# Attention of a hybrid decoder layer, written in units of 128 keys with the projection stream between them

## The chip, the cores and the metric

The kernel runs on one core of one Trainium2 chip. The metric is device microseconds of one execution; the median of several runs counts. One further execution was recorded by the hardware profiler, and all rows below come from it.

## The reference

One decoder layer for 512 tokens of width 1024: two token mixers side by side (HGRN2, a gated recurrence, and NSA, a sparse attention), merged by gates, followed by an MLP. The change touches the attention and the projections that are computed beside it. With 512 tokens and blocks of 64 keys the top-16 selection takes every block, and the window of 512 covers every earlier token, so that the selected and the window branch are both causal softmax attention over all earlier keys, with keys and values of their own (ks, vs and kw, vw).

```python
def reference(x, ...):
    u = rms_norm(h, norm_pre_mix[i])
    proj = u @ w_in[i]
    hq, hf, hi, hg, nq, nkv, ngate, ga, gb = jnp.split(proj, SPLIT_POINTS, axis=-1)
    kc, vc, ks, vs, kw, vw = jnp.split(nkv, 6, axis=-1)
    y_a = hgrn2_mixer(hq, hf, hi, hg, ...)
    y_b = nsa_mixer(nq, kc, vc, ks, vs, kw, vw, ngate, ...)
...
def nsa_mixer(...):                      # 16 heads in 4 groups of 4, 64 wide
    s = jnp.einsum('bgrqd,bgnd->bgrqn', qb, k_cmp)      # compressed keys
    o_cmp = jnp.einsum('bgrqn,bgnd->bgrqd', masked_softmax(s, ...), v_cmp)
    s = jnp.einsum('bgrqd,bgqkd->bgrqk', qr, kg)        # selected keys
    o_sel = jnp.einsum('bgrqk,bgqkd->bgrqd', masked_softmax(s, m_sel), vg)
    s = jnp.einsum('bgrqd,bgkd->bgrqk', qr, kwb)        # window
    o_win = jnp.einsum('bgrqk,bgkd->bgrqd', masked_softmax(s, m_win), vwb)
    out = gt[:, :, 0] * o_cmp + gt[:, :, 1] * o_sel + gt[:, :, 2] * o_win
```

## The kernel before

**Precision.** A float32 operand is held as two tiles of a faster type, a high part (`hi`) and the rest (`lo`). A product of two such operands takes three matmuls, a triple (hi·hi, lo·hi, hi·lo). Making the pair costs a copy on ScalarE (ACT) and a subtraction on VectorE (DVE): `split`, L59 and L60. During the attention weights are made into pairs in another way, `split_by_transfer`, L62 to L65: two copies on ACT and a transfer with accumulation, issued on GpSimd's queue (POOL).

**The main stream.** `job_n` (L136) multiplies the 512 normalised tokens (`uh`, `ul`) with 256 columns of `w_in`: four token tiles t, each with eight k-steps of a triple with 256 columns, in a PSUM bank of the pool `mainp` (two banks). It needs two chunks of weights. `job_t` (L129) makes 128 columns transposed: eight k-steps of a triple with 512 columns, one chunk. Three chunks can live at a time (`PAIRS`), and two raw ones (`RAWS`). Beside the attention run five `job_n` (queries of groups 1 to 3; keys and values of the second pair of groups, twice) and eight `job_t` (`gate_tanh`, L218).

**The attention.** `attend` (L469) does one of four groups of heads as a generator of eight steps: for each tile t of 128 queries the two branches. `scores` (L472) of a step: matmuls against t+1 tiles of keys, the maximum on DVE (L488), the exponentials on ACT (L492), the scaling (L502, L505). `values` (L508): for each of the t+1 tiles of keys four transposes of the probabilities (L169), the split into `pth` and `ptl` (ACT, then DVE), and two matmuls (L515, L516). One such tile of keys is called a unit here: 20 in a group, 80 in all. The scores of a step are written ahead of the values of the step before it. At the end of a t stands one more matmul (L542) and `store`.

**Pieces.** A group's queries and keys are made ready by short pieces: `tr_r` (L351) transposes into a `mainp` bank and a copy to SBUF (keys L379, queries L415), two more transposes (L424), the compressed scores with their softmax (`cmp_soft`, L431), and four times transposes and a split of their probabilities (`cmp_probs`, L455).

**Order.** The framework plans each engine's order ahead of time: among the instructions that are ready in the plan it takes the one that is written first in the program. An engine then executes in that order. `mark` (L76) notes matmuls of the attention, and `spread` (L79) puts the first matmul of each k-step of the stream behind one of them, in proportion: a bound on how early it may come. From L618 the program writes some steps of the attention first, then a few jobs of the stream, spread over these steps, then the pieces of the next group, and so on; the last steps of one group are written alternating with the first steps of the next (`advance`, L611). The list of marks is not emptied before this part, so that the first job, `kv(1, 0)`, is spread over marks of the stage ahead of the attention too. The attention's PSUM banks come free when those of the stage ahead (`prp`) are released, after the last `cmp_probs` of group 0.

Of the kernel before, what the change touches and what calls it, by code (L numbers as in the profile page):

```python
# [19 lines left out]
NT = 4  # L20
NK = 8
# [7 lines left out]
def hybrid_layer(ctx: ExitStack, tc: tile.TileContext, x, p, w_in, w_branch_a, w_branch_b, w_out,  # L29
# [120 lines left out]
    def n_chunks(w, cols, rows=(4, 4)):  # L150
        res, k = [], 0
# [206 lines left out]
    def kv_job(pr, ck, cv, kdst, vdst, chunks=None):  # L358
# [16 lines left out]
        job_n(chunks or n_chunks(w_in, [(ck + pr * 128, 128), (cv + pr * 128, 128)]),  # L375
              (uh, ul), mainp, evac)
        for j in range(2):
            for src, dst, e in ((hn, KH, 0), (ln, KL, 1)):
                ps = tr_r([src[:, t, j] for t in range(NT)])  # L379
                kt = kdst[2 * j + e]  # L380
                if e:
                    act.copy(kt, ps.bitcast(FT))
                else:
                    dve.tensor_copy(kt, ps)
                dst.append(kt)
        return KH, KL, V

    def q_job(g):
        return q_rest(*q_main(g))

    def q_main(g):
        qsn = ns.tile([128, NT, 4, 128], FR, name="stage", bufs=1)
# [14 lines left out]
        cols = [(C_NQ + g * 256, 256)]  # L407
        job_n(n_chunks(w_in, cols) if g else n_chunks(w_in, cols + [(C_GATE, 48)], (3, 3, 2)),
# [3 lines left out]
    def q_rest(qsn, qn):  # L412
        qs = [ns.tile([128, 512], FR, name="qs", tag="qs", bufs=8) for _ in range(4)]
# [6 lines left out]
        qt = []  # L420
# [8 lines left out]
        return qs, qt  # L429

    def cmp_soft(g, qt):  # L431
# [6 lines left out]
        sc = ns.tile([128, NT, 4, 32], FT, name="sc")  # L438
# [16 lines left out]
    def cmp_probs(sc):  # L455
        chl = []
# [10 lines left out]
        return chl  # L467

    def attend(g, qs, chl, kvs):  # L469
# [38 lines left out]
        def values(t, br, Ps, py):  # L508
            V = kvs[br][2]
            for kt in range(t + 1):  # L510
# [5 lines left out]
                mark(pe.matmul(py, V[j][:, kt], lo, start=False, stop=False), 1.0)  # L516

        def store(t, py):
# [16 lines left out]
        for i, (t, br) in enumerate(steps):  # L535
# [3 lines left out]
            values(t, br, pend, py)  # L539
# [736 lines left out]
```

## Time and profile before

| what | us |
|---|---|
| median of 3 runs (1232.16 to 1237.37) | 1235.8 |
| the profiled execution | 1233.28 |
| its span, first to last instruction | 1231.5 |
| the attention in it, first score to last value matmul | 136.5 to 411.5 |

The profile lists for each engine when it was busy. PE is TensorE's matmul, PEld its weight loads. A matmul's row has its whole duration, although the next one starts before it ends: the interval from one start to the next is the time that a stream of matmuls takes. Behind a row or group stands the idle time of the engine before it, and what ended that.

### The profile page before, as it was taken

What the parts mean: (1) busy time and instruction counts of PE and PEld (TensorE: products, weight loads), DVE (VectorE), ACT (ScalarE), POOL (GpSimd) and SP (SyncE); (2) the same over time, 40 slices, a digit from 0 to 9 for tenths busy, and PEclk for the clock granted to TensorE, in tenths of its full rate; (3) what the DMA queues carried; (4) which work ended last, traced back from release to release, by engine and by line L of the source; (5) the groups of instructions that cost most, each with busy time, mean ns of one, the idle gap of its engine ahead of it and who ended that gap; (6) DMA issues with size and microseconds to landing.
All of it is one profiled execution on the core that took longest, in us unless ns stands there. A gap on an engine that the chain in (4) does not pass through costs nothing.

```text
span 1231.5 us, 18849 instructions
## 1 busy us (share of the span) xinstructions
PE 1190.6 (97%) x7183; PEld 1041.3 (85%) x7183; DVE 782.9 (64%) x1411; ACT 642.1 (52%) x1294; POOL 145.2 (12%) x282
## 2 busy tenths in 40 slices
PE   7999899998999999999999999999999999999997
PEld 6898797887878889898988788888989889889886
DVE  6774667837788367777776454579527447555664
ACT  5555777847887334444444222367637427336442
POOL 2021131321311110101010201010000000000000
PEclk9999999999999999999999999999999999999999
DMA  6337534252522431313132894535414324227401
GB/s 179 103 93 178 144 77 104 43 130 54 126 60 73 142 104 50 88 52 86 52 86 77 240 239 152 173 118 170 140 35 128 113 69 140 83 69 239 155 18 69
DMA packets 134333, 137.08 MB, mean 111 GB/s; under 512 B 8881, under 2 KB 108385, under 8 KB 134242
## 3 DMA queue, kind: packets, MB, share of 16 engines
q1 hardware_dynamic: 119776, 106.44, 29.7%
q0 software_dynamic: 5792, 19.93, 7.3%
q10 hardware_dynamic: 8674, 9.51, 2.3%
q8 instruction: 56, 0.92, 0.3%
q14 instruction: 35, 0.29, 0.1%
HBM read 111.73 MB, written 14.68 MB: 103 GB/s over the span
## 4 chain that ended last, share of the span: by engine, by line
PE 68%; DVE 3%; ACT 1%; issue 1%; DMA 0%; POOL 0%; SPq 0%; POOLq 0%; ACTq 0%; DVEq 0%
PE up L1065 11%; PE ps L91 6%; PE ps L92 6%; PE ps L93 6%; PE acc L1151 5%; PE acc L1150 5%; PE acc L1152 5%; PE lev L736 3%; PE acc L942 3%; PE acc L944 2%; PE acc L943 2%; PE ps L146 2%; PE ps L144 2%; PE ps L145 2%; PE tr L1065 2%; PE tr L169 1%
## 5 line engine op out<-in xcount | busy, mean ns | idle before, releaser
L59 ACT CAST whi<-raw 128x1024 fp32r<-128x1024 f32 (+1 forms) x181 | 188.4, 1046 | 205.6 <-PE acc L1152 59.1
L60 DVE TENSOR_TENSOR wlo<-raw,whi 128x1024 fp32r<-128x1024 f32 (+1 forms) x181 | 221.6, 1229 | 114.9 <-ACT whi L59 113.7
L144 PE MATMUL ps<-whi,uh 128*128 128x256 f32 (+1 forms) x512 | 148.6, 292 | 6.2 <-ACT uh L59 2.9
L145 PE MATMUL ps<-wlo,uh 128*128 128x256 f32 (+1 forms) x512 | 147.8, 289 | 0.3 <-DVE wlo L60 0.2
L146 PE MATMUL ps<-whi,ul 128*128 128x256 f32 (+1 forms) x512 | 147.6, 289 | 0.0
L91 PE MATMUL ps<-uh,whi 128*128 128x512 f32 x288 | 118.0, 410 | 0.2 <-DVE chl L466 0.2
L93 PE MATMUL ps<-uh,wlo 128*128 128x512 f32 x288 | 114.9, 399 | 0.1
L92 PE MATMUL ps<-ul,whi 128*128 128x512 f32 x288 | 115.0, 399 | 0.0
L144 PEld LDWEIGHTS ps<-whi,uh 128*128 128x128 f32 x512 | 97.9, 192 | 9.3 <-ACT uh L59 3.5
L1151 PE MATMUL acc<-wlo,fh 128*128 128x512 f32 x256 | 101.3, 396 | 0.0
L1150 PE MATMUL acc<-whi,fh 128*128 128x512 f32 x256 | 100.6, 395 | 0.0
L1152 PE MATMUL acc<-whi,fl 128*128 128x512 f32 x256 | 100.0, 395 | 0.0
L145 PEld LDWEIGHTS ps<-wlo,uh 128*128 128x128 f32 x512 | 98.3, 192 | 1.5 <-DVE wlo L60 0.6
L146 PEld LDWEIGHTS ps<-whi,ul 128*128 128x128 f32 x512 | 98.1, 192 | 0.5 <-DVE ul L60 0.2
L492 ACT ACTIVATE P<-ps_s,nm 128x128 f32<-128x128 f32 (+3 forms) x128 | 67.7, 538 | 16.3 <-DVE nm L488 12.6
L60 DVE TENSOR_TENSOR ptl<-tr,pth 128x512 fp32r<-128x512 f32 x82 | 55.1, 684 | 25.0 <-ACT pth L59 24.4
L488 DVE TENSOR_REDUCE nm<-ps_s 128x1 f32<-128x384 f32 (+3 forms) x88 | 55.5, 634 | 23.9 <-PE ps_s L486 23.4
L484 PE MATMUL ps_s<-kt,qs 128*128 128x128 f32 (+3 forms) x256 | 60.1, 336 | 5.3 <-ACT P L492 5.1
L93 PEld LDWEIGHTS ps<-uh,wlo 128*128 128x128 f32 x288 | 54.3, 188 | 12.3 <-DVE wlo L60 0.3
L91 PEld LDWEIGHTS ps<-uh,whi 128*128 128x128 f32 x288 | 54.3, 189 | 10.6 <-PE py L542 0.6
L92 PEld LDWEIGHTS ps<-ul,whi 128*128 128x128 f32 x288 | 54.4, 189 | 10.1
L59 ACT CAST pth<-tr 128x512 fp32r<-128x512 f32 x82 | 47.5, 592 | 24.8 <-PE tr L169 23.8
(324 smaller groups left out, 2921.1 us busy)
## 6 DMA issues: line engine op xcount, KB each, us to landing
raw<-in_w_in_dram SPq DMA_DIRECT2D x58, 512.0 KB, 3.9
raw<-in_w_up_dram SPq DMA_DIRECT2D x32, 512.0 KB, 3.8
raw<-in_w_down_dram SPq DMA_DIRECT2D x32, 512.0 KB, 4.4
wlo<-raw POOLq DMA_DIRECT2D x18, 512.0 KB, 4.7
raw<-in_w_in_dram SPq DMA_DIRECT2D x17, 256.0 KB, 3.8
raw<-in_w_branch_a_dram SPq DMA_DIRECT2D x8, 512.0 KB, 9.3
raw<-in_w_branch_b_dram SPq DMA_DIRECT2D x32, 128.0 KB, 6.9
raw<-in_w_out_dram SPq DMA_DIRECT2D x8, 512.0 KB, 5.4
```

Of the source, the lines that this page charges most:

```text
L59: act.copy(hi, src)
L60: return dve.tensor_sub(lo, src, hi)
L91: rec.append(pe.matmul(ps, lh, rh, start=first, stop=False).ins)
L92: pe.matmul(ps, lh, rl, start=False, stop=False)
L93: pe.matmul(ps, ll, rh, start=False, stop=last)
L144: rec.append(pe.matmul(o, stat[0][:, k, s], hi[:, i], start=(k == 0), stop=False).ins)
L145: pe.matmul(o, stat[0][:, k, s], lo[:, i], start=False, stop=False)
L146: pe.matmul(o, stat[1][:, k, s], hi[:, i], start=False, stop=(k == NK - 1))
L1065: pe.matmul(ps[:, c], l[:, k, cs], r[:, k], start=f and n == 0, stop=e and n == 2, skip_group_check=True)
L1150: pe.matmul(ps, fh[:, k % 4, s], hi[:, k % 2], start=(k == 0), stop=False)
L1151: pe.matmul(ps, fh[:, k % 4, s], lo[:, k % 2], start=False, stop=False)
L1152: pe.matmul(ps, fl[:, k % 4, s], hi[:, k % 2], start=False, stop=(k == NK - 1))
```

## The change

The attention's generator now gives way after each unit, not after each step. Between two units the program writes one piece (if one is due) and then as many k-steps of the stream as keep 288 weighted steps (a triple with 256 columns counts 1, one with 512 columns 2) in proportion to 80 units, 3.6 a unit. The first matmul of a k-step is put behind the last mark. A chunk of weights is prepared (loaded and made into a pair) where an older one has been used up, three at a time. The groups follow each other; only the next group's first scores are written three units ahead of a group's end. The marks are emptied before the attention. The tiles `stage` have two buffers, `sc` one, and `yl` takes the place of `ytmp`.

```diff
+    def after(m):
+        tc.add_manual_dep(m.ins, marks[-1][0].name, mybir.DependencyInfo(
+            mybir.DependencyClass.NoSync, mybir.DependencyReason.DATA), reason="stream")
+
+    def stream_n(chunks, evac, ahead):
+        for t in range(NT):
+            ps = mainp.tile([128, 512], FT, name="ps", tag="main")
+            s = slice(t * 128, t * 128 + 128)
+            k = 0
+            for c, (hi, lo) in enumerate(chunks):
+                o = ps[:, :hi.shape[2]]
+                for i in range(hi.shape[1]):
+                    m = pe.matmul(o, uh[:, k, s], hi[:, i], start=(k == 0), stop=False)
+                    after(m)
+                    pe.matmul(o, uh[:, k, s], lo[:, i], start=False, stop=False)
+                    pe.matmul(o, ul[:, k, s], hi[:, i], start=False, stop=(k == NK - 1))
+                    k += 1
+                    yield 1
+                ahead(t == 3 and c + 1)
+            evac(t, o)
+
+    def stream_t(pair, evac, ahead):
+        ps = mainp.tile([128, 512], FT, name="ps", tag="main")
+        hi, lo = pair
+        for k in range(NK):
+            m = pe.matmul(ps, hi[:, k], uh[:, k], start=(k == 0), stop=False)
+            after(m)
+            pe.matmul(ps, hi[:, k], ul[:, k], start=False, stop=False)
+            pe.matmul(ps, lo[:, k], uh[:, k], start=False, stop=(k == NK - 1))
+            yield 2
+        ahead(1)
+        evac(ps)
...
-        st = ns.tile([128, 2, NT, 2, 128], FR, name="stage", bufs=1)
+        st = ns.tile([128, 2, NT, 2, 128], FR, name="stage", bufs=STAGES)
...
+        def keys():
+            for j in range(2):
+                for src, dst, e in ((hn, KH, 0), (ln, KL, 1)):
+                    ps = tr_r([src[:, t, j] for t in range(NT)])
+                    kt = kdst[2 * j + e]
+                    if e:
+                        act.copy(kt, ps.bitcast(FT))
+                    else:
+                        dve.tensor_copy(kt, ps)
+                    dst.append(kt)
+                    yield True
+        return (KH, KL, V), keys(), evac
...
+    def queries(g, qm, qs, chl):
+
+        qt = []
+        yield from q_rest(*qm, qs, qt)
+        sc = cmp_soft(g, qt)
+        yield True
+        yield from cmp_probs(sc, chl)
...
-            yl = at.tile([128, 512], FR, name="yl", bufs=1)
             act.copy(yh[a], tmp[a])
+            yl = tmp.bitcast(FR)
...
+            units = values(t, br, pend, py)
             pend = nxt
-            if br:
-                pe.matmul(py, vch[:, t % 2, g], chl[t // 2], start=False, stop=True)
-                store(t, py)
-            yield True
-
-    def together(*gens):
-        live = list(gens)
-        while live:
-            live = [g for g in live if next(g, None) is not None]
+            for kt in range(t + 1):
+                next(units)
+                if br and kt == t:
+                    pe.matmul(py, vch[:, t % 2, g], chl[t // 2], start=False, stop=True)
+                    store(t, py)
+                yield True
...
-    a0 = attend(0, q0, c0, (k0, k1))
-    advance(a0, 7)
-    kb = kv(1, 0)
-    gate_tanh(C_GB, gB_d, gp, 3, 4)
-    q1 = q_main(1)
-    spread(.9)
+    jobs = [("q", 1), ("kv", 0), ("q", 2), ("kv", 1), ("gate", C_GB, gB_d, 3), ("q", 3)]
+    jobs += [("gate", C_GB, gB_d, m) for m in range(4, 8)] + [("gate", C_GA, gA_d, m) for m in range(3)]
+    def chunk_list(job):
+        if job[0] == "gate":
+            return [lambda: w_simple(w_in, 0, NK, job[1] + job[3] * 128, 128)]
+        cols = [(C_NQ + job[1] * 256, 256)]
+        if job[0] == "kv":
+            cols = [((C_KS, C_KW)[job[1]] + 128, 128), ((C_VS, C_VW)[job[1]] + 128, 128)]
+        return [lambda k=k: n_chunks(w_in, cols, (4,), k)[0] for k in (0, 4)]
+    todo = [(i, f) for i, job in enumerate(jobs) for f in chunk_list(job)]
+    ready = {i: [] for i in range(len(jobs))}
+    live = [0]
+    def prepare():
+        while todo and live[0] < 3:
+            i, f = todo.pop(0)
+            ready[i].append(f())
+            live[0] += 1
+    def ahead(done):
+        if done:
+            live[0] -= 1
+        prepare()
+    pieces, kb = [], [None, None]
+    group = {0: (q0, c0)}
+    def main_stream():
+        for i, job in enumerate(jobs):
+            if job[0] == "gate":
+                def evac(ps, job=job):
+                    tg = gp.tile([128, 512], FT, name="gt", tag="gt")
+                    act.activation(tg, ps, AF.Tanh, scale=0.5)
+                    act.dma_start(job[2][job[3]], tg)
+                yield from stream_t(ready[i][0], evac, ahead)
+            elif job[0] == "kv":
+                kb[job[1]], keys, evac = kv(1, job[1], stream=True)
+                yield from stream_n(ready[i], evac, ahead)
+                pieces.insert(0, keys)
+            else:
+                qsn, qn, evac = q_main(job[1], True)
+                yield from stream_n(ready[i], evac, ahead)
+                group[job[1]] = [], []
+                pieces.append(queries(job[1], (qsn, qn), *group[job[1]]))
+    total, used, n = 288, [0], [0]
+    stream = main_stream()
+    def units(a, count):
+        for _ in range(count):
+            next(a)
+            n[0] += 1
+            while pieces:
+                if next(pieces[0], None):
+                    break
+                pieces.pop(0)
+            while used[0] < total * n[0] / 80:
+                w = next(stream, None)
+                if w is None:
+                    break
+                used[0] += w
     marks.clear()
+    prepare()
+    a = attend(0, *group[0], (k0, k1))
+    next(a)
+    for g in range(4):
+        units(a, 17)
+        nxt = None
+        if g < 3:
+            nxt = attend(g + 1, *group[g + 1], (k0, k1) if g == 0 else kb)
+            next(nxt)
+        units(a, 3)
+        a = nxt
+    whole(stream)
...
```

## Rows read from the trace of the kernel before

**Rows 1.** the page: span; two transfers: KB each, us from issue to landing

```profile
span 1231.5 us, 18849 instructions
...
wlo<-raw POOLq DMA_DIRECT2D x18, 512.0 KB, 4.7
yl_d<-yl POOLq DMA_DIRECT2D x16, 128.0 KB, 2.5
```

**Rows 2.** stretches: us, then PE PEld DVE ACT POOL busy, clock, DMA, GB/s

```profile
140.00:152.00 12.00, 10.29 (x65) 7.85 (x63) 10.12 (x29) 11.51 (x40) 1.95 (x6) 1.00 0.66 136
152.00:185.00 33.00, 32.84 (x220) 29.90 (x220) 22.98 (x52) 25.73 (x63) 10.34 (x22) 1.00 0.37 87
350.00:373.00 23.00, 19.73 (x118) 14.98 (x118) 21.69 (x46) 18.83 (x55) 3.82 (x4) 1.00 0.29 67
136.50:411.50 275.00, 258.93 (x1654) 219.99 (x1652) 199.18 (x431) 208.71 (x526) 64.97 (x117) 0.99 0.36 83
```

**Rows 3.** matmul groups of the attention: count, busy, mean ns, idle before

```profile
L484 PE MATMUL ps_s<-kt,qs 128*128 128x128 f32 (+3 forms) x256 | 60.1, 336 | 5.3 <-ACT P L492 5.1
L169 PE MATMUL tr<-ident,P 128*128 128x128 f32 x320 | 53.1, 279 | 2.9 <-DVE P L502 2.5 <-ACT P L505 0.3
L144 PE MATMUL ps<-whi,uh 128*128 128x256 f32 x140 | 40.4, 289 | 0.0
L516 PE MATMUL py<-ptl,V 128*128 128x512 f32 x80 | 35.8, 448 | 2.2 <-DVE ptl L60 1.9
L91 PE MATMUL ps<-uh,whi 128*128 128x512 f32 x64 | 27.7, 433 | 0.2 <-DVE chl L466 0.2
L486 PE MATMUL ps_s<-causal,identr 128*128 128x128 f32 (+2 forms) x88 | 22.3, 253 | 0.0
L354 PE MATMUL trr<-identr,stage 128*128 128x128 f32 x80 | 11.7, 251 | 2.5 <-ACT stage L370 1.2 <-DVE V L60 1.1
L542 PE MATMUL py<-chl,vch 128*128 128x512 f32 x16 | 6.7, 417 | 0.0
L460 PE MATMUL pct<-ident,sc 128*32 128x128 f32 x48 | 6.6, 273 | 0.0
L436 PE MATMUL pc<-bd,qt 128*128 128x64 f32 x48 | 5.8, 274 | 0.0
L424 PE MATMUL trq<-ident,qn 128*128 128x128 f32 x24 | 3.6, 273 | 0.0
```

**Rows 4.** matmuls in order of time: start, us, what

```profile
163.24 0.28 PE L144 MATMUL ps<-whi,uh 128*128 128x256 f32 x1
163.35 0.40 PE L515 MATMUL py<-pth,V 128*128 128x512 f32 x1
163.59 0.28 PE L145 MATMUL ps<-wlo,uh 128*128 128x256 f32 x1
...
167.24 1.04 PE L169 MATMUL tr<-ident,P 128*128 128x128 f32 x8
168.03 0.36 PE L146 MATMUL ps<-whi,ul 128*128 128x256 f32 x1
```

**Rows 5.** matmul groups ahead of the attention, 121 to 136.5

```profile
L144 PE MATMUL ps<-whi,uh 128*128 128x256 f32 x28 | 8.8, 313 | 1.8 <-ACT gt L222 1.8
L460 PE MATMUL pct<-ident,sc 128*32 128x128 f32 x16 | 2.1, 273 | 0.0
```

**Rows 6.** one copy of a weight chunk in order of time on ACT

```profile
125.39 1.04 ACT L63 CAST whi<-raw 128x1024 fp32r<-128x1024 f32 x1 [3.96 <-DMA raw<-in_w_in_dram]
```

**Rows 7.** ACT and DVE groups of the attention

```profile
L492 ACT ACTIVATE P<-ps_s,nm 128x128 f32<-128x128 f32 (+3 forms) x128 | 67.7, 538 | 16.3 <-DVE nm L488 12.6 <-DVE r L496 1.3 <-PE tr L169 0.9
L59 ACT CAST pth<-tr 128x512 fp32r<-128x512 f32 x80 | 46.4, 592 | 20.4 <-PE tr L169 19.4 <-PE trr L354 0.7
L64 ACT ACTIVATE wlo<-whi 128x1024 fp32r<-128x1024 f32 x15 | 16.2, 1078 | 0.0
L60 DVE TENSOR_TENSOR ptl<-tr,pth 128x512 fp32r<-128x512 f32 x80 | 53.9, 684 | 22.0 <-ACT pth L59 21.3
```

More of the change, by code (lines that the diff above doesn't have):

```diff
@@ L148, in job_n, with n_chunks @@
             evac(t, o)
-    def n_chunks(w, cols, rows=(4, 4)):
-        res, k = [], 0
+    def n_chunks(w, cols, rows=(4, 4), k=0):
+        res = []
         for nk in rows:
@@ L374, in evac, with whole, q_main @@
                 split(V[j][:, t, 0:64], V[j][:, t, 64:128], s)
[L375 to L392, printed above, removed]
+        if stream is None:
+            job_n(chunks or n_chunks(w_in, [(ck + pr * 128, 128), (cv + pr * 128, 128)]),
+                  (uh, ul), mainp, evac)
+        def keys():
[10 more added lines that the diff above has]
+        return (KH, KL, V), keys(), evac
+    def whole(*gens):
+        for gen in gens:
+            for _ in gen:
+                pass
+    def q_main(g, stream=False):
+        qsn = ns.tile([128, NT, 4, 128], FR, name="stage", bufs=STAGES)
         qn = ns.tile([128, NT, 256], FT, name="qn", bufs=1)
@@ L407, in q_main @@
         cols = [(C_NQ + g * 256, 256)]
+        if stream:
+            return qsn, qn, evac
         job_n(n_chunks(w_in, cols) if g else n_chunks(w_in, cols + [(C_GATE, 48)], (3, 3, 2)),
@@ L410, in q_main, with q_rest @@
         return qsn, qn
-    def q_rest(qsn, qn):
-        qs = [ns.tile([128, 512], FR, name="qs", tag="qs", bufs=8) for _ in range(4)]
+    def q_rest(qsn, qn, qs, qt):
+        qs += [ns.tile([128, 512], FR, name="qs", tag="qs", bufs=8) for _ in range(4)]
         for h in range(4):
@@ L453, in cmp_soft, with cmp_probs @@
         return sc
-    def cmp_probs(sc):
-        chl = []
+    def cmp_probs(sc, chl):
         for t in range(NT):
@@ L558, in hybrid_layer, with kv @@
     kv_dst = [kv_tiles(ns)]
-    def kv(pr, br, chunks=None):
-        return kv_job(pr, (C_KS, C_KW)[br], (C_VS, C_VW)[br], kv_dst[pr][0][br], kv_dst[pr][1][br], chunks)
+    STAGES = 2
+    def kv(pr, br, chunks=None, stream=None):
+        return kv_job(pr, (C_KS, C_KW)[br], (C_VS, C_VW)[br], kv_dst[pr][0][br], kv_dst[pr][1][br], chunks, stream)
     gp = tc.alloc_tile_pool(name="gp", reuse_waits="tile", bufs=2)
-    k0 = kv(0, 0, first_chunks)
+    k0, keys, _ = kv(0, 0, first_chunks)
+    whole(keys)
     kcd = cmp_load(0)
@@ L588, in hybrid_layer @@
     vcd = cmp_load(1)
-    k1 = kv(0, 1)
+    k1, keys, _ = kv(0, 1)
+    whole(keys)
     ph = cmp_core(0, kcd)
-    q0, qt0 = q_job(0)
+    q0, qt0, c0 = [], [], []
+    whole(q_rest(*q_main(0), q0, qt0))
     gate_tanh(C_GB, gB_d, gp, 0, 1)
@@ L596, in hybrid_layer @@
     cmp_out(1, ph)
-    c0 = cmp_probs(sc0)
+    whole(cmp_probs(sc0, c0))
     gate_tanh(C_GB, gB_d, gp, 1, 2)
@@ L609, in hybrid_layer @@
     rec.clear()
-    def advance(a, na, b=None, nb=0):
-        for i in range(max(na, nb)):
-            if i < na:
-                next(a, None)
-            if i < nb:
-                next(b, None)
-    a0 = attend(0, q0, c0, (k0, k1))
-    advance(a0, 7)
-    kb = kv(1, 0)
-    gate_tanh(C_GB, gB_d, gp, 3, 4)
-    q1 = q_main(1)
-    spread(.9)
-    marks.clear()
-    rec.clear()
-    gate_tanh(C_GB, gB_d, gp, 4, 5)
-    q1, qt1 = q_rest(*q1)
-    spread(1)
-    c1 = cmp_probs(cmp_soft(1, qt1))
@@ L630, in hybrid_layer @@
-    spread(1)
-    a1 = attend(1, q1, c1, (k0, k1))
-    advance(a0, 3, a1, 6)
-    kb = kb, kv(1, 1)
-    q2 = q_main(2)
-    spread(1)
-    marks.clear()
-    rec.clear()
-    gate_tanh(C_GB, gB_d, gp, 5, 6)
-    q2, qt2 = q_rest(*q2)
-    spread(1)
-    c2 = cmp_probs(cmp_soft(2, qt2))
-    spread(1)
-    a2 = attend(2, q2, c2, kb)
-    advance(a1, 4, a2, 7)
-    gate_tanh(C_GB, gB_d, gp, 6, 7)
-    q3 = q_main(3)
-    spread(.8)
-    marks.clear()
-    rec.clear()
-    gate_tanh(C_GB, gB_d, gp, 7, 8)
```

24 lines of the change are left out of this document (6 added, 18 removed).

## The prediction

> **What bounds the kernel now.** I read the stretches first. From 136.5 to 411.5 us TensorE (PE) is idle for 16.1 of 275 us by the profile, ACT is busy for 209 and DVE for 199 [rows 2]: three engines near their limits, none at it. But a matmul's row lasts longer than the time to the next start (0.28 us for 256 columns, yet 0.11 us to the next start) [rows 4], so each wait hides part of itself. The groups and the intervals give the work proper. One matmul takes 0.10 us with up to 128 columns (eight transposes in 0.79 us), 0.11 us with 256, 0.24 us with 512 [rows 4]. The groups [rows 3] hold 584 matmuls with up to 128 columns (320 + 80 + 48 + 48 + 24, and 64 of L486): 58 us. The triples with 256 columns, 140 of each of L144 to L146: 46 us. The wide ones (80 each of L515 and L516, 16 of L542, 64 each of L91 to L93), 368 in all: 88 us. The scores, 64 each of 128, 256, 384 and 512 columns: 40 us. The rest of L486: 4 us. Together 236 us: **39 us are lost in the attention**. Where? From 152 to 185 us, where triples of the stream stand between the attention's matmuls [rows 4], PE idles for 0.16 of 33 us. From 140 to 152 and from 350 to 373 us, where the list in order of time has no triple, it idles for 1.7 of 12 and 3.3 of 23 us, with ACT or DVE busy for over 90% [rows 2]. The stream is used up in some places and missing in others, and the attention alone is bound by ACT and DVE.
>
> **The change, part by part.**
>
> Moved into the attention: the first job. In front of the attention 28 triples of `kv(1, 0)` run between 121 and 136.5 us, where only 16 transposes of `cmp_probs` are due otherwise [rows 5]. With the marks emptied, no triple can come before the first value matmul. They move: 28 x 3 x 0.11 = 9 us. The 15.5 us in front shrink to the chain: two `cmp_probs` and their copies, twice. A chl copy by ACT and a subtraction by DVE take about as long as those of a unit, 0.59 and 0.68 us [rows 7], two of each overlap in some 1.9 us, and eight transposes take 0.8 us: twice 2.7, so I take 6 us. Bounds: 4 us, if the second pair's transposes lie beside the first pair's copies, and 10 us, if ACT is held by a weight copy that waits for its transfer, as it was for 3.96 us [rows 6]; what is queued behind it are these copies, and the attention's banks wait for them.
>
> Work in the attention: 140 + 28 triples are 8 more than the five jobs' 160: the next stage's, 8 x 3 x 0.11 = 3 us, drawn forward. So 236 + 9 - 3 = 242 us, with 3 us to follow behind it.
>
> What is lost there after the change, in four terms. **Order within a pair of units.** A unit's lump of stream, 3.6 triples or 3.6 x 3 x 0.11 = 1.2 us, is written ahead of the next unit's transposes, and is ready as soon as the unit's last matmul is out; so by the planner's rule it goes first. Two `tr` banks let two units be under way. I expect: two lumps, then two units' transposes, then a wait of 0.59 + 0.68 us for the copies [rows 7], in which PE has the second unit's transposes (0.4 us) and one hi matmul (0.24 us). That leaves 0.63 us in each of 40 pairs, 25 us. Scores (40 us of L484 and 10 us of L486, 1.25 us a pair) go first wherever a bank is free, and can fill it. Bounds: 0, if they or the pieces always do, and 25 us, if never; and more, if exponentials stand ahead of the copies (a rival, below). I take half, 12 us, since scores stand at the beginning of a step and fill the first pairs of it. **First steps of a group.** With one or two units in a step, the chain from scores over maximum, exponentials and scaling is longer than the units that cover it; before, these steps were written beside the long ones of another group. The nearest rows are the two stretches with such steps, with 1.7 and 3.3 us idle [rows 2]: 2.5 us for each of four groups, 10 us (7 to 13). **Weights.** A job's second chunk can be made only when the first chunk of the job before is used up, 8 triples ahead of its need, 2.2 units or 7 us at 3.4 us a unit. It costs two copies of 1.08 us [rows 7] and a transfer of 4.7 us [rows 1], 6.9 us. It just fits; whatever ACT does first is exposed. Four such places, 0 to 1.5 us each: 2 us. POOL issues these transfers in order behind the rotations and the `yl` subtractions, but is busy for 65 of 275 us [rows 2]; SP has only the raw loads. **Pieces.** One behind each unit, 41 in all: their matmuls are in the work, their copies in ACT's and DVE's. The first transposes of a piece can wait for the evacuation; before, 2.5 us for five jobs [rows 3]. I keep 2.5 us.
>
> At no cost: two `stage` buffers (the pieces of one job may now lie behind the next job's evacuation), one `sc`; and `yl` in `ytmp`: a `store` must now wait for the last one's transfer, 2.5 us [rows 1], but the nearest two lie two units, some 7 us, apart. If POOL were late by over 4 us, ACT would stand there.
>
> **The sum.** Before, from 121 to 411.5 us: 290.5 us. After: 6 + 242 + (12 + 10 + 2 + 2.5) + 3 = 275.5. Starts are read to 0.01 us; with 0.12 us for 256 columns the work would be 4 us more, and the time after as much, so I take 3 us of it: 278.5. **12 us less.** Behind it the next stage is bound by PE, so the gain goes through. The profiled execution took 1233.3 us, with 1.8 us around its span; it would take 1221. The median lies 2.5 us above it: **1224 us**, with 1216 to 1231 for this case alone.
>
> At L354 PE stood still for 2.5 us [rows 3], with the stream's triples written behind it. A rule of the Trainium skill speaks against the change here: "TensorE: Matmul & The Clock Gate", under "Step-by-step: what each phase is for", says that PE pulls only weight loads ahead and that matmuls stay in program order. By that rule a lump that is planned too early delays what stands behind it with no remedy on the chip, and the third rival's time comes out; if PE could pull matmuls ahead, it would be the first rival's. The wait at L354 agrees with the rule.
>
> **The rivals.**
>
> *All waits covered.* Everywhere the mix is that of 152 to 185 us, with 0.16 us idle in 33 us; only the first steps cost their 10 us. Then 11.5 us are lost instead of 26.5: 15 us less than forecast, **1209 us**. For it: that stretch has long steps and 3 to 5 triples a unit. Against it: there the stream had the lower rank, and filled; here it leads.
>
> *No difference.* The gain is paid back at the edges: ACT held in front of the attention (10 instead of 6 us), first steps at 13, weights at 6: 11 us more, **1235 us**. For it: the wait of 3.96 us [rows 6], which the three chunks prepared ahead of the attention repeat.
>
> *Slower: lumps hold the transposes back.* The pair's wait is never filled, 25 instead of 12 us, and in every other pair an exponential of 0.54 us [rows 7] stands on ACT ahead of the copies, 20 x 0.54 = 11 us: 24 us more than forecast, **1248 us**. It decides from 0.6 us a pair on, where the forecast's 12 us are gone. For it: ACT is busy for 76% already [rows 2], and the attention does not shrink it. Against it: during two lumps ACT and DVE have 2.4 us to work ahead.
>
> **How the numbers follow.** About 0.5%, 6 us, can be told from no change here. Forecast 0.40, of which 0.32 lies below 1229.6 us; covered 0.20; no difference 0.17; slower 0.23. Faster 0.52, the same 0.25, slower 0.23. The range goes from 1208 to 1247 us: half of the covered case and half of the slower one lie outside, 0.2.
>
> **What would show it.** The attention's first score at about 127 us, not 136.5. In order of time on PE: lumps of 3 to 4 whole triples behind L516, then two units' transposes, then a short wait for `pth` or `ptl`. No stretch of 20 us without triples, and PE's idle time spread evenly, highest at the four groups' first steps. ACT busy for nearly 80% in the attention. The forecast is wrong if waits for `ptl` come behind most units (slower), if there are none (covered), or if the attention starts at 131 us or later with ACT waiting for a raw chunk.

## The result: slower, by 13 us

The changed kernel took 1246.97 us (median of 4 runs, 1244.86 to 1250.86) against 1233.98 us for the kernel before beside it: 1.0116 times, 95% interval 1.0094 to 1.0138. The forecast was 1224 us. The time lies at the upper end of the range, 1247, and nearest to the rival with lumps, 1248, but by luck: the runs below show that another cause made it.

The profiled execution took 1250.9 us. Its span, to set beside [rows 1], and its stretches, to set beside [rows 2] (us, then PE, PEld, DVE, ACT and POOL busy, granted clock, DMA share, GB/s):

```profile
span 1249.1 us, 18862 instructions
```

```profile
120.00:130.00 10.00, 3.39 (x21) 2.32 (x19) 2.91 (x7) 5.13 (x9) 0.64 (x1) 0.69 0.67 161
130.00:141.00 11.00, 10.81 (x45) 9.56 (x44) 7.94 (x21) 7.49 (x30) 0.23 (x1) 0.50 0.43 97
140.00:165.00 25.00, 24.49 (x177) 23.00 (x177) 20.68 (x48) 19.83 (x53) 7.95 (x16) 0.98 0.10 22
200.00:225.00 25.00, 20.99 (x131) 16.50 (x129) 22.35 (x49) 20.85 (x52) 6.96 (x10) 1.00 0.37 78
225.00:266.00 41.00, 37.30 (x261) 34.27 (x260) 24.82 (x51) 27.62 (x61) 14.30 (x32) 0.92 0.38 87
266.00:306.00 40.00, 32.20 (x207) 27.58 (x206) 20.39 (x55) 24.01 (x67) 6.55 (x16) 0.91 0.35 74
129.70:425.20 295.50, 273.19 (x1735) 237.38 (x1734) 202.21 (x443) 213.19 (x538) 70.06 (x129) 0.96 0.35 81
```

The attention now goes from 129.7 to 425.2 us, where it went from 136.5 to 411.5: it starts 7 us earlier and lasts 20 us longer. Of the 20, 9 are the 28 triples that moved in. Four stretches carry most of the rest. In front, 120 to 141 us, TensorE (PE) is first idle and then at half its clock: 0.50 is the 1.2 GHz level. From 140 to 165 us all is as it was meant, PE idle for 0.5 of 25 us. From 200 to 225 us the attention runs bare, DVE busy for 22 of 25 us and PE for 21. From 225 to 266 us PE is idle for 3.7 of 41 us, at a mean clock of 0.92. From 266 to 306 us it is idle for 8 of 40 us, with no engine near its limit.

The front in order of time, ACT's rows and then PE's (start, us, what, and in brackets the idle time before it with what ended it):

```profile
125.39 1.04 ACT L63 CAST whi<-raw 128x1024 fp32r<-128x1024 f32 x1 [4.44 <-DMA raw<-in_w_in_dram]
126.34 0.59 ACT L222 ACTIVATE gt<-ps 128x512 f32<-128x512 f32 x1
126.83 0.56 ACT L506 CAST chl<-pct 32x512 fp32r<-32x512 f32 x1
...
120.51 1.04 PE L501 MATMUL pct<-ident,sc 128*32 128x128 f32 x8
128.16 1.89 PE L501 MATMUL pct<-ident,sc 128*32 128x128 f32 x8 [6.61 <-DVE chl L507]
129.70 1.09 PE L533 MATMUL ps_s<-kt,qs 128*128 128x128 f32 x4
```

The weight copy of [rows 6] still waits for its load, and the `chl` copies stand behind it. Before, the 28 triples of [rows 5] ran meanwhile; now PE has nothing and stands for 6.6 us.

PE's waits (us in total, times, longest), first from 140 to 200 us, then from 200 to 306 us:

```profile
PE py L564 <- ACT pth L59: 0.6, 1, 0.6
PE py L565 <- DVE ptl L60: 0.5, 1, 0.5
PE ps_s L533 <- ACT P L541: 0.2, 1, 0.2
```

```profile
PE trr L354 <- DVE V L60: 3.4, 2, 1.8
PE pct L501 <- POOL sc L494: 3.2, 1, 3.2
PE py L564 <- ACT pth L59: 2.6, 4, 1.5
PE ps_s L533 <- ACT P L541: 2.6, 3, 1.8
PE tr L169 <- DVE knat L401: 1.3, 1, 1.3
PE py L565 <- DVE ptl L60: 1.1, 3, 0.6
```

In the first 60 us the waits come to 1.3 us, although pieces stand there too: group 1's queries, transposed from 168 us on, in time for that group's first units at 198 us. In the 106 us after that they come to 15.2 us, where they come to 8.8 us in the same stretch of the kernel before; the two largest stand at the pieces' own transposes. The longest gap between two units lies here. PE's rows in it, with the last value matmuls of units 41 and 42 at the ends:

```profile
273.13 0.49 PE L565 MATMUL py<-ptl,V 128*128 128x512 f32 x1 [0.57 <-DVE ptl L60]
276.79 0.61 PE L501 MATMUL pct<-ident,sc 128*32 128x128 f32 x4 [3.17 <-POOL sc L494]
...
284.00 0.56 PE L354 MATMUL trr<-identr,stage 128*128 128x128 f32 x4 [1.62 <-DVE V L60]
...
292.58 0.46 PE L354 MATMUL trr<-identr,stage 128*128 128x128 f32 x4
...
304.13 0.50 PE L565 MATMUL py<-ptl,V 128*128 128x512 f32 x1
```

Unit 42 comes 31 us after unit 41. It is the first that needs the keys of `kv(1, 1)`, and these are transposed only from 284 to 293 us. In the kernel before they are transposed from 241 to 252 us, ahead of the queries of the same group (265 to 273 us).

One measure goes through all that follows. I take the time from each matmul's start to the next, less the lower quartile of its line and shape in the whole trace, and call the sum what a stretch loses; a half clock counts in it as well as a wait. The kernel before loses 3.9 us from 120 to 140 us and 41.5 from 140 to 440; the changed kernel 13.0 and 47.5. That is 15 of the 17.6 us by which the two spans differ; the profiled execution of the changed kernel was the slowest of its four, 4 us over their median. Of the 47.5, 7.8 us fall between 200 and 225 us, 8.7 between 225 and 266, and 13.6 between 266 and 306, where the kernel before loses 6.1, 6.5 and 7.8.

A second count shows how the stream keeps its plan: the weighted steps that have begun at a unit's last value matmul, against those planned up to that unit (3.6 a unit). A lag of up to 4 is the unit's own share, which follows. In the changed kernel it is no more than that up to unit 10; it grows from the first piece on, at 168 us, and is 40 at unit 40.

### The profile page after: what moved, and what is told of

Read it like the earlier page. It is cut to its first block, busy times and chain, and to the rows that moved or that the text cites. A ratio compares the mean times of both kernels' runs of the same rounds, so it can differ in the third digit from the quotient of the medians.

```text
span 1249.1 us, 18862 instructions
## 1 busy us (share of the span) xinstructions
PE 1195.0 (96%) x7183; PEld 1047.5 (84%) x7183; DVE 782.0 (63%) x1411; ACT 644.5 (52%) x1294; POOL 148.4 (12%) x282
## 4 chain that ended last, share of the span: by engine, by line
PE 81%; DVE 6%; ACT 5%; DMA 4%; issue 2%; POOL 1%; SPq 1%; ACTq 0%; POOLq 0%; DVEq 0%
PE up L1146 11%; PE ps L91 6%; PE ps L92 5%; PE ps L93 5%; PE acc L1232 5%; PE acc L1231 5%; PE acc L1233 5%; PE lev L817 3%; PE ps L144 3%; PE ps L146 3%; PE ps L145 3%; PE tr L169 3%; PE acc L1023 2%; PE acc L1025 2%; PE acc L1024 2%; PE ps_s L533 2%
## 5 line engine op out<-in xcount | busy, mean ns | idle before, releaser
L144 PE MATMUL ps<-whi,uh 128*128 128x256 f32 (+1 forms) x352 | 101.2, 289 | 6.3 <-ACT uh L59 3.8
L145 PE MATMUL ps<-wlo,uh 128*128 128x256 f32 (+1 forms) x352 | 101.1, 288 | 0.2 <-DVE wlo L60 0.2
L146 PE MATMUL ps<-whi,ul 128*128 128x256 f32 (+1 forms) x352 | 101.1, 287 | 0.0
L91 PE MATMUL ps<-uh,whi 128*128 128x512 f32 x224 | 90.1, 402 | 0.0
L537 DVE TENSOR_REDUCE nm<-ps_s 128x1 f32<-128x384 f32 (+3 forms) x88 | 55.4, 636 | 29.6 <-PE ps_s L535 29.1
L144 PEld LDWEIGHTS ps<-whi,uh 128*128 128x128 f32 x352 | 66.5, 190 | 8.5 <-ACT uh L59 4.4
L145 PEld LDWEIGHTS ps<-wlo,uh 128*128 128x128 f32 x352 | 66.8, 190 | 0.6 <-DVE wlo L60 0.5
L146 PEld LDWEIGHTS ps<-whi,ul 128*128 128x128 f32 x352 | 66.7, 190 | 0.3 <-DVE ul L60 0.2
L59 ACT CAST pth<-tr 128x512 fp32r<-128x512 f32 x82 | 47.5, 589 | 29.1 <-PE tr L169 28.3
L1233 PEld LDWEIGHTS acc<-whi,fl 128*128 128x128 f32 x256 | 48.2, 188 | 11.2
L1231 PEld LDWEIGHTS acc<-whi,fh 128*128 128x128 f32 x256 | 48.0, 188 | 11.3
L1232 PEld LDWEIGHTS acc<-wlo,fh 128*128 128x128 f32 x256 | 48.1, 188 | 11.1
```

The lines of the kernel that those rows point to most:

```text
L59: act.copy(hi, src)
L91: rec.append(pe.matmul(ps, lh, rh, start=first, stop=False).ins)
L144: rec.append(pe.matmul(o, stat[0][:, k, s], hi[:, i], start=(k == 0), stop=False).ins)
L145: pe.matmul(o, stat[0][:, k, s], lo[:, i], start=False, stop=False)
L146: pe.matmul(o, stat[1][:, k, s], hi[:, i], start=False, stop=(k == NK - 1))
L1231: pe.matmul(ps, fh[:, k % 4, s], hi[:, k % 2], start=(k == 0), stop=False)
```

## The experiments

Each run stood beside runs of the kernel before, whose median lay between 1232.2 and 1233.0 us each time (beside the changed kernel it was 1234.0, so differences to that in us are uncertain by 1 or 2). Ratios are to those, with the 95% interval.

### The front

**e2_front**: the first 28 steps ahead of the attention.

```
 def after(m):
+    if not marks:
+        return
...
-            while used[0] < total * n[0] / 80:
+            while used[0] < first + (total - first) * n[0] / 80:
...
     prepare()
+    first = 28
+    while used[0] < first:
+        used[0] += next(stream)
```

> The changed kernel, but the first 28 steps of the stream are written ahead of the attention and put behind nothing, the rest spread over the 80 units (3.25 a unit). Theory F: the idle 6.6 us ahead of the attention and the slow clock behind it go, 8 to 12 us, to 1235 to 1239 us. Theory P: only what lies ahead of the attention changes, and the pieces' waits stay, so not below 1235 us. Theory L: lumps are a tenth smaller, 1 to 2 us, 1245 us.

Measured: 1236.45 us, 1.0031 (1.0019 to 1.0044), 10.5 us less than the changed kernel. Its front:

```profile
120.00:130.00 10.00, 8.73 (x68) 7.88 (x68) 3.49 (x7) 5.63 (x11) 2.37 (x6) 1.00 0.81 198
130.00:141.00 11.00, 9.56 (x74) 8.51 (x71) 6.82 (x20) 8.95 (x33) 3.20 (x10) 1.00 0.56 124
```

139 matmuls in these 21 us instead of 63, and the clock at 2.4 GHz throughout. The first score comes at 134.4 us, 4.7 later, and the time is still shorter: 28 triples of 9 us stand in the front, and the half clock is gone.

**e11_before_nofront**: the same from the other side, in the kernel before.

```
+    marks.clear()
     a0 = attend(0, q0, c0, (k0, k1))
     advance(a0, 7)
```

> The kernel before with one edit: the places collected in the front (the compressed probabilities' and the first scores' transposes and matmuls) are forgotten when the attention starts, so that the 64 triples of kv(1,0), q(1) and the gate are spread over the attention of group 0 from its second unit on and none stands in the front, as in the changed kernel. Theory F (work of the stream in the front hides its chain of waits and holds the clock up): 7 to 10 us more than 1234, 1241 to 1244. If the front's waits cost nothing that the attention doesn't give back: 1232 to 1236.

Measured: 1240.33 us, 1.0061 (1.0038 to 1.0084): 7.9 us more. An empty front costs 8 us in a kernel that has nothing else of the change; the triples that stood there are spread over group 0's attention. It loses 9.9 us from 120 to 140 us, where the kernel before loses 3.9, and behind that no more than it (40.6 and 41.5).

**e10_two_chunks**: one chunk fewer ahead of the attention.

```
+    live[0] = 1
     prepare()
+    live[0] = 2
```

> The changed kernel with two chunks of weights prepared ahead of the attention instead of three; the third is loaded, copied and subtracted after the stream's first four steps. Theory A (ScalarE is held by the copy of the third chunk, which waits 4.4 us for its load at 125 us, and the compressed probabilities' copies stand behind it): the first score comes 3 to 4 us earlier and the time is 3 to 5 us less, 1242 to 1244. Theory F without A (the front is short of TensorE work and runs at the half clock, whatever ScalarE does): 0 to 1 us less.

Measured: 1249.82 us, 1.014 (1.0113 to 1.0167), no gain. It settles nothing. The copy that holds ACT is that of the third chunk, the first of `kv(1, 0)`; written later in the program, it still came at the same place in ACT's order:

```profile
125.16 1.04 ACT L63 CAST whi<-raw 128x1024 fp32r<-128x1024 f32 x1 [4.06 <-DMA raw<-in_w_in_dram]
```

**e18_chl_first**: the hold itself taken away, in the kernel of e16_fast_pin_bank (below; 1230.6 us).

```
 def split_by_transfer(hi, lo, src):
-    act.copy(hi, src)
+    behind(act.copy(hi, src), last_chl[0], "chl")
```

> The kernel of e16_fast_pin_bank (1230.6) with the copies of the weight chunks prepared ahead of the attention ordered on ScalarE behind group 0's last copy of compressed probabilities. In e16_fast_pin_bank ScalarE stands 4.0 us at the second chunk's copy, which waits for its load, and those copies stand behind it; e10_two_chunks left that chunk where it was. Theory A (that hold is what the front loses): the first score comes some 5 us earlier and the time is 4 to 6 us less, 1224 to 1227. Theory F without A (the front is short of TensorE work and its half clock costs as much whenever the chain ends): the score comes earlier, and the time is 0 to 2 us less, 1228 to 1231.

Measured: 1234.24 us, 1.0016 (0.9995 to 1.0038): no gain, rather 3.7 us more. PE's row, then ACT's:

```profile
123.83 1.09 PE L539 MATMUL ps_s<-kt,qs 128*128 128x128 f32 x8
...
124.70 1.99 ACT L65 CAST whi<-raw 128x1024 fp32r<-128x1024 f32 x2
128.51 0.35 ACT L547 ACTIVATE P<-ps_s,nm 128x128 f32<-128x128 f32 x1
138.56 1.04 ACT L65 CAST whi<-raw 128x1024 fp32r<-128x1024 f32 x1 [4.03 <-DMA raw<-in_w_in_dram]
```

The first score comes at 123.8 us instead of 128.9, and from 120 to 141 us the clock is granted at a mean of 0.91 instead of 0.67. But the weight copies now stand ahead of the first exponentials, and the third chunk's copy, which held ACT in e16 (not the second's, as the expectation says), waits 4.0 us among them. By the fifth unit's value matmul the lead is lost (153.8 us against 152.4). The hold moved to the next consumer: taken away in this way, it gains nothing.

### Order within a step

**e3_transposes_first**: the next unit's transposes ahead of this unit's value matmuls.

```
-            for kt in range(t + 1):
+            coming = turned(0)
+            for kt in range(t + 1):
+                hi, lo = coming
+                coming = turned(kt + 1) if kt < t else None
```

> The changed kernel, but within a step the transposes and the split of unit k+1 are written ahead of the value matmuls of unit k, and so ahead of its lump of stream. Theory L: the waits for pth and ptl behind the lumps go, 12 to 24 us, to 1223 to 1235 us. Theories P and F: the stretches in which the stream runs lose nothing now, so within 4 us of the changed kernel, 1243 to 1251 us.

Measured: 1248.16 us, 1.0132 (1.0106 to 1.0159), no gain. Taken alone it proves little: of the some 1850 matmuls between 120 and 440 us, the two kernels' sequences agree in 98%, so the planner had already drawn the transposes ahead. Its row, beside that of the changed kernel above:

```profile
140.00:165.00 25.00, 24.49 (x178) 23.04 (x177) 20.54 (x48) 19.84 (x54) 7.93 (x16) 0.98 0.10 22
```

What speaks against the lumps is the trace of the changed kernel: `pth` and `ptl` were waited for 7.5 us in 14 places between 121 and 430 us, not 25 us and more. And from 140 to 165 us, where the stream runs in its lumps as planned, the changed kernel loses 1.5 us.

### The pieces

**e12_no_pieces** and **e13_front_no_pieces**: the pieces of groups 1 to 3 left out, in the changed kernel and in e2_front.

```
-                pieces.insert(0, keys)
+                kb[job[1]] = (k0, k1)[job[1]]
...
-                group[job[1]] = [], []
-                pieces.append(queries(job[1], (qsn, qn), *group[job[1]]))
+                group[job[1]] = q0, c0
```

> The changed kernel without the pieces: groups 1 to 3 take group 0's queries and compressed probabilities and pair 0's keys and values, so the transposes of queries and keys, the compressed scores' softmax and their transposes of groups 1 to 3 are left out; the stream's matmuls, copies and weights stay. The left-out TensorE work is about 18 us by the trace of the changed kernel, start to start (80 transposes of 0.065 us, 24 of 0.1, 48 small matmuls of 0.11, 48 transposes of 0.109). If the pieces cost only their own TensorE work: 1247 - 18 = 1229. Theory P (the steps stand behind waiting pieces, so that the attention runs bare there and the stream alone later): another 10 to 20 us less, 1209 to 1219.

> The kernel of e2_front with the same pieces left out as in e12_no_pieces. If the pieces cost their TensorE work alone: 1236.5 - 18 = 1218. Theory P: 1200 to 1210. If front and pieces are two losses that add, it lies as far under e12_no_pieces as e2_front lies under the changed kernel, 10 us.

Measured: 1211.78 us (0.9855, 0.9809 to 0.9901) and 1205.74 us (0.9796, 0.9775 to 0.9817): 35.2 us under the changed kernel, and 30.7 under e2_front. With 18 us for the pieces' matmuls, they cost 17 and 13 us beside. Some of that is their copies on ACT and DVE, which are left out too; e9 and e16 below, which have all pieces, bound that part. In e12, with the pins and banks of the changed kernel, the stream never lags by more than 4 steps. From 140 to 440 us it loses 24 us, where the changed kernel loses 47.5 and the kernel before 41.5. So the units by themselves do lose less than before, by 17 us, and the pieces take all of it. By these traces they take 6 us more, but that is no more than what the two profiled executions are off their medians (3.9 us over in the changed kernel, 2.6 under in e12). Front and pieces do not quite add: e13 lies 6 us under e12, not 10.

**e1_pin_units** and **e4_pin_front**: each step pinned behind its own unit's last value matmul; in e4 with e2's front.

```
-        tc.add_manual_dep(m.ins, marks[-1][0].name, mybir.DependencyInfo(
+        tc.add_manual_dep(m.ins, behind_unit[0].name, mybir.DependencyInfo(
...
+                behind_unit[0] = last.ins
```

> The changed kernel, but a k-step of the stream is put behind the last value matmul of its unit, not behind the last mark, which can be the transposes of a piece. Theory P (the stream stands still with every piece that waits, and the attention goes on without filler): most of the loss of the stretches from 165 to 300 us and from 350 to 385 us goes, 10 to 20 us, to 1227 to 1237 us, and the stream keeps within some 8 weighted steps of its plan instead of 40. Theory L (a unit's lump of stream stands ahead of the next unit's transposes): the lumps stay, so within 3 us of the changed kernel, 1244 to 1250 us. Theory F (the triples that are missing ahead of the attention): no change either, 1244 to 1250 us.

> The edits of the first two kernels together. Theories P and F together: the two gains add, 18 to 30 us, to 1217 to 1229 us, below the kernel before (1234). Theory L: not below 1243 us.

Measured: 1242.81 us, 1.008 (1.0065 to 1.0095), and 1237.33 us, 1.0027 (1.0012 to 1.0041). The pins alone give 4 us, and on top of the front nothing: both below what was expected. In e1's trace the stream lags by up to 20 steps, where 8 were expected; while pieces are written it comes in blocks of eight steps, a whole bank tile, with two to four units between them.

**e5_bank** and **e6_py1**: the pieces get a bank of their own, which `py` gives up; e6 is the control, with the `py` line alone.

```
-            py = nsp.tile([128, 512], FT, name="py", tag="py")
+            py = nsp.tile([128, 512], FT, name="py", tag="py", bufs=1)
...
-    trp[:] = [mainp, "main"]
+    trp[:] = [nsp, "piece", 1]
```

> The changed kernel with one PSUM bank kept for the pieces (transposes of queries, keys, compressed probabilities), so that they no longer take turns with the stream's tiles in its two banks; that bank is taken from the output accumulator py, which has one instead of two. Theory B (the stream stands because a piece holds one of its two banks until DVE or ACT has read it): 5 to 10 us less than the changed kernel's 1247, i.e. 1237 to 1242, less what the single py costs, which e6 shows. Theory P (the steps stand because each is pinned behind the last piece's transposes): no more than 3 us less, 1244 to 1248. Theory F (the front) says nothing of this part.

> The control of e5_bank: the changed kernel with one py bank and nothing in the bank that comes free. Each of the 16 query tiles must then have its output read by ACT and DVE before the next tile's first value matmul: 0 to 0.5 us each, so 0 to 8 us more than 1247. What e5_bank gains by theory B is read against this run, not against the changed kernel.

Measured: 1249.01 us, 1.0134 (1.0116 to 1.0152), and 1252.92 us, 1.0175 (1.0152 to 1.0198). The single `py` costs 6 us and the bank gives 4 back.

**e9_pin_front_bank** and **e15_front_bank**: the bank with e4's edits, and with e2's.

> The kernel of e4_pin_front (1237) with e5_bank's edit: steps pinned behind their own unit, 28 steps ahead of the attention, a bank of its own for the pieces, one py bank. The single py cost 6 us in e6_py1 and the piece bank gave 4 back in e5_bank. Theory B (with the pins behind the units the shared banks are what still stops the stream, in blocks of eight steps): the bank gives back more than it costs, 1228 to 1234. If the gain of the pins and of the front do not add for another reason: 1238 to 1242.

> The kernel of e2_front (1236.5) with a bank of its own for the pieces and one py bank; the steps still pinned behind the last mark, pieces' transposes among them. Two gates one behind the other: the pins still hold the steps and the single py costs its 6 us less the 4 that the bank gives, 1237 to 1241. If the bank alone was what e9_pin_front_bank gained by: 1225 to 1229.

Measured: **1225.14 us**, 0.9944 (0.9925 to 0.9964), and 1235.89 us, 1.0029 (1.0013 to 1.0045). With the front filled, pins alone gave nothing (e4: 1237.3) and the bank alone nothing (e15: 1235.9); together they give 11 to 12 us. They are two gates one behind the other: a step of the stream waits for its pin and for a bank, and a late piece holds both. The traces show it: the stream lags its plan by up to 24 steps in e4 and 36 in e15, and by no more than 4 in e9. e9 beats the kernel before by 0.6%, with all pieces in it and at the price of the single `py`.

### Due times

**e7_pin_bank**: pins and bank without the front.

> The changed kernel with its steps pinned behind their own unit and a bank of its own for the pieces (one py bank), and nothing ahead of the attention. Pins alone gave 4 us (e1_pin_units, 1242.8), the bank alone gave 4 against its control, and its one py bank costs 6. If pins and bank are two gates one behind the other (a step goes only when both are open), together they give what neither gives alone: 1231 to 1236, some 10 us over e9_pin_front_bank for the front. If they are two separate losses, 1247 - 4 - 4 + 6: 1243 to 1246.

Measured: 1247.71 us, 1.0123 (1.0106 to 1.014). The gates alone were not it. PE's rows around unit 41, the last value matmuls of units 41 and 42 at the ends, and the stretch between:

```profile
270.30 0.40 PE L567 MATMUL py<-ptl,V 128*128 128x512 f32 x1
...
271.83 0.28 PE L376 MATMUL ps<-whi,ul 128*128 128x256 f32 x1
276.08 1.03 PE L503 MATMUL pct<-ident,sc 128*32 128x128 f32 x4 [3.98 <-POOL sc L496]
278.50 1.03 PE L503 MATMUL pct<-ident,sc 128*32 128x128 f32 x4 [1.38 <-DVE chl L509]
280.91 0.75 PE L354 MATMUL trr<-identr,stage 128*128 128x128 f32 x4 [1.38 <-DVE chl L509]
282.45 0.75 PE L354 MATMUL trr<-identr,stage 128*128 128x128 f32 x4 [0.79 <-DVE kt L423]
...
295.22 0.50 PE L567 MATMUL py<-ptl,V 128*128 128x512 f32 x1
```

```profile
271.00:289.00 18.00, 9.80 (x52) 7.52 (x50) 5.15 (x9) 4.81 (x12) 3.85 (x4) 0.61 0.37 87
```

The stream keeps its plan here, 144 weighted steps at unit 41, and just so there is nothing left to run: the pieces of group 2 come one after the other, each behind the copy of the one before, group 2's scores behind them, and the clock goes down to a mean of 0.61. The plan itself is late. `kv(1, 1)` is full after 128 of 288 steps, at unit 36; its keys and the rest of q(2)'s pieces are then written behind units 36 to 42, and group 2 scores with those keys from unit 41 on. That each piece waits for the copy of the one before is also the work of their single bank: e1, whose pieces share two banks with the stream, loses 10.1 us from 266 to 306 us, where e7 loses 18.7. How much of that the bank makes, no run separates.

**e16_fast_pin_bank** and **e17_fast**: the stream written faster up to unit 35, in e7_pin_bank and in the changed kernel.

```
-            while used[0] < total * n[0] / 80:
+            while used[0] < min(4.6 * n[0], 160 + (n[0] - 35) * 128 / 45):
```

> The kernel of e7_pin_bank (1247.7) with the stream written faster at first: 4.6 weighted steps a unit up to unit 35 and 2.8 after that, instead of 3.6 throughout; the same steps, nothing ahead of the attention. Theory D (due times: in e7_pin_bank the stream keeps its plan, but its plan brings the pieces of group 2 only just ahead of that group's first scores, and unit 42 comes 25 us after unit 41): most of the some 18 us lost there from 260 to 300 us goes, and the front's loss stays, 1233 to 1238. If what e9_pin_front_bank has over e7_pin_bank (22.6 us) all comes from the matmuls in the front themselves: 1245 to 1249.

> The changed kernel with e16_fast_pin_bank's faster first part alone; pins and banks as in the changed kernel. Theory D alone (due times are what the pieces cost): 1235 to 1240. Theory D with the gates (written earlier, the steps are still held behind the pieces' transposes and by the shared banks, as e15_front_bank and e4_pin_front were): 1242 to 1248.

Measured: 1230.57 us, 0.9981 (0.9959 to 1.0002), and 1241.46 us, 1.007 (1.0045 to 1.0094). One line of arithmetic takes 17 us off e7, with the front as empty as it was. Units 41 and 42 in e16, and the stretch from 266 to 306 us in e7, e16 and e9:

```profile
288.37 0.40 PE L567 MATMUL py<-ptl,V 128*128 128x512 f32 x1
...
291.23 0.45 PE L567 MATMUL py<-ptl,V 128*128 128x512 f32 x1
```

```profile
266.00:306.00 40.00, 29.45 (x177) 24.55 (x176) 23.02 (x51) 21.89 (x59) 7.05 (x10) 0.79 0.25 60
```

```profile
266.00:306.00 40.00, 36.12 (x245) 31.95 (x245) 31.02 (x72) 30.05 (x84) 11.28 (x23) 0.96 0.36 83
```

```profile
266.00:306.00 40.00, 36.86 (x241) 32.61 (x240) 28.67 (x66) 31.18 (x84) 11.87 (x24) 0.96 0.38 79
```

2.9 us from unit to unit instead of 24.9, and 245 matmuls in the stretch instead of 177. A part of the wait only moved: unit 43 comes at 301.2 us in e16 and at 300.2 in e7, so from unit 41 to 43 it is 12.8 us instead of 29.9. In the changed kernel the same line gives 5.5 us, since the gates still hold the steps: they lag by up to 48. So the 28 steps ahead of the attention work twice: they fill the front, and they bring every later job five units nearer to its due time (128 steps at unit 31).

**e8_front_kv1** and **e14_all**: `kv(1, 1)` as the third job, in e2_front and in e9_pin_front_bank.

```
-    jobs = [("q", 1), ("kv", 0), ("q", 2), ("kv", 1), ("gate", C_GB, gB_d, 3), ("q", 3)]
+    jobs = [("q", 1), ("kv", 0), ("kv", 1), ("q", 2), ("gate", C_GB, gB_d, 3), ("q", 3)]
```

> The kernel of e2_front (28 steps of the stream ahead of the attention, 1236.5) with one more edit: the second key and value job, kv(1,1), is the stream's third job instead of its fourth, so that its keys are there some nine units before group 2 scores with them. Theory K (what is lost around 260 to 320 us is group 2 waiting for these keys): 4 to 6 us less than e2_front, 1230 to 1233. If the pieces cost the same wherever they stand: 1235 to 1238.

> The kernel of e9_pin_front_bank (1225.1) with e8_front_kv1's order of jobs, kv(1,1) third. Theory K as in e8_front_kv1, which lies 7 us under e2_front: another 4 to 7 us, 1218 to 1221. If what e8_front_kv1 gained was the stream's delay behind the pieces, which pins and bank have already taken away: 1223 to 1227.

Measured: 1229.19 us, 0.9981 (0.9966 to 0.9996), and 1227.44 us, 0.9962 (0.9948 to 0.9976). Where the gates hold the stream back, earlier keys give 7 us; where they don't, nothing more (e9 and e14 overlap). The order of the jobs is a third way to the same slack.

## Why the prediction was wrong

By its own steps, of which two failed, the front's and the pieces':

- **The front.** Forecast 6 us, between 4 and 10, with the first score at 127 us. It came at 129.7, 9.2 us after the start of the first pair's transposes, for the reason that the upper bound named: ACT held at L63. That is some 3 us. The step that failed was to cost the front in waits alone. PE's clock was granted at a mean of 0.92 from 120 to 141 us before, with the triples; without them it fell, and 11 us at 0.50 (130 to 141 us) give half of them away, 5 us more. Together 8 us, as e11 measured it; e2 gained 10, some of it probably by earlier due times. The Trainium skill, "TensorE: Matmul & The Clock Gate", under "HAM oscillation — how this bites in real kernels", warns of this in a loop that waits for a transfer each time: the work behind the wait starts at the lower clock. The rows agree, 6.6 us of waiting and then 0.50, and the forecast didn't draw on it.
- **Order, first steps, weights.** Forecast 12, 10 and 2, together 24 us. e12_no_pieces, which has these and no pieces, loses 24 us from 140 to 440 us. The sum held, perhaps by luck: how it divides was not measured, and with waits of 1.3 us from 140 to 200 us the share of the order is probably smaller than 12.
- **Pieces.** Forecast 2.5 us, measured 13 to 17. This is the largest miss, and the step was the choice of the row: L354's 2.5 us [rows 3] is what transposes waited in a kernel that wrote them well ahead of their use. (Nearly all of it is two waits at 244 and 246 us, at the keys of `kv(1, 1)`, some 20 us before the queries of the same group are transposed.) The forecast counted the pieces, their matmuls and their copies, and never set the unit at which a piece is ready beside the unit at which it is due. The diff and the unit of 3.4 us would have given it: 128 / 3.6 is unit 36, the keys are used at unit 41, and between lie some 17 us for an evacuation, four transposes of keys with their copies, and the rest of q(2)'s softmax and transposes, one behind each unit.
- **What stands behind a late piece.** Not in the forecast at all: the stream's steps, pinned behind the piece's transposes and in the same two banks. It is why the stream was missing just where the attention was bare (200 to 225 us) and was made up where nothing covered it (29 steps between units 41 and 42).
- **The sum.** Its terms were added wrongly: 6 + 242 + 26.5 + 3 is 277.5, not 275.5, so that the forecast by its own terms is 1226. With 13 to 17 for the pieces instead of 2.5, and 8 more for the front, that is 1245 to 1249; measured 1247.
- **Moved work, `yl` in `ytmp`, `stage`, `sc`.** The 28 triples moved as said, 160 of L371 in the attention. The 8 of the next stage stayed in it instead of following behind, which the sum counts the same. ACT waited 1.4 us in all for a `yl_d` transfer.
- **The rivals.** The slower one gave the right time, by luck, with a mechanism that the trace doesn't show: few waits for `pth` or `ptl`. "No difference" had the right place, ACT's hold in front, and too small a price. The rule on PE's order that stood beside the forecast (the Trainium skill, "TensorE: Matmul & The Clock Gate", "Step-by-step: what each phase is for") agrees with this trace, though not for lumps: at 276.8 us PE stood 3.2 us before a `pct` transpose (the row of the waits above), with nine matmuls of the stream next in order. At the two waits of L354 that the forecast took for it, value matmuls were next, not triples.
- **The signs of being wrong.** None came that clearly: waits for `ptl` stood in 6 places only, and the first score at 129.7 us, short of 131. No sign looked at the pieces.

Open: how much of the 17 us of e12 is the pieces' copies rather than waits. e9 has all pieces, pays about 6 us for its single `py` and loses 32.5 us from 140 to 440 us, so the copies and what is left of the waits come to some 2 us over the 24 of e12; with e16, which loses 29.1, they come to nothing. That is an estimate from a few traces, not a measurement.

## What to carry to other kernels

When work is cut into pieces and spread evenly, write two numbers beside each piece: the unit at which its input is complete and the unit at which its result is used; a plan that is even in steps can be late for a piece, and one line that fills earlier was worth 17 us where the gates were open, and 5.5 where they were not. Filler must not wait for what it is to cover: pin it to the work that it accompanies, not to the last thing written, and give short-lived transposes a bank of their own, because either gate alone held it as well as both; but both opened together gave nothing (e7) until the pieces were also in time. And don't take the matmuls out of a chain of waits unless the chain goes too: here they delayed the first score by 4.7 us, and without them the 9 us had to be done elsewhere and 5 more went to the lower clock.

## What was not expected of the hardware

A single wait of 6.6 us was followed by 11 us at the granted 0.50, although PE's rows are busy for 10.8 of these 11 us; in e2_front, with 139 matmuls in the same 21 us, it stayed at 1.00. So PE's busy share said nothing of the clock here: at the half clock each row lasts longer and fills the time, and only the column of the granted clock and the count of matmuls (45 against 74) show the difference.

The kernel before has a shorter case of the same, at the wait of 1.8 us in [rows 5], which ends at 127.0 us:

```profile
127.00:130.00 3.00, 3.00 (x14) 3.00 (x15) 1.56 (x3) 2.29 (x5) 1.48 (x4) 0.50 0.41 119
```

There the clock was back at 1.00 from 131 us on.
